# Moving operands at chosen offsets from the weights, modulo 128 bytes, in a two-layer fp32 block

## The chip, the cores and the metric

The kernel runs on one core of one Trainium2 chip. The time is the device time of one execution in microseconds; several executions are taken and the median is given. Profiled executions carry their own time, beside the span from their first to their last instruction.

## The reference

A block of two layers works on 256 tokens of 2048 features in float32; at the end stands an RMS norm. Layer 0 has a mixer with a convolution branch and a pooling branch, layer 1 a short-convolution mixer; each is followed by a SwiGLU of hidden size 5632. Cut to what matters:

```python
def conv_pool_mixer(x, ...):               # layer 0
    u = rms_norm(x, norm_g) @ w_in         # 2048 -> 3072
    a = a_val * sigmoid(a_gate)            # 1024 features: 31-tap causal convolution, layer norm, silu
    p = multiscale_pool(b_in, w_pool, ...) # 1024 features in four groups, four windows
    return concatenate([a, p]) @ w_out     # 2048 -> 2048

def short_conv_mixer(x, ...):              # layer 1
    u = rms_norm(x, norm_g) @ w_in         # 2048 -> 6144
    y = gate_b * causal_depthwise_conv(gate_c * v, conv_w)
    return y @ w_out                       # 2048 -> 2048

def swiglu(h, w_gate, w_up, w_down):       # 2048 -> 5632 (twice) -> 2048
    return (silu(h @ w_gate) * (h @ w_up)) @ w_down

for i in range(2):
    h = h + mixer_i(h)
    h = h + swiglu(rms_norm(h, ffn_norm[i]), w_gate[i], w_up[i], w_down[i])
return rms_norm(h, final_norm)
```

## The kernel before

Features lie on the 128 partitions, tokens along the free dimension (T = 256), so the weights are the stationary operand of each matmul and the activations the moving one. All weights are cut into blocks of 128 x 128 and stored in the order in which they are used. Units of 16 blocks come from HBM through one queue into the tile `w`; each piece of 8 blocks is then split into two fp32r tiles, `hi` by a cast on ScalarE (line 114) and `lo`, the rest, by a subtraction on VectorE or, in a part of the first mixer, on GpSimd (line 121). There are 4 buffers of `w`, and 6 each of `hi` and `lo`.

An activation is split in the same way: a chunk of 128 features takes 2 x 256 columns of fp32r, the high parts and then the low parts. The tiles that matmuls stream as moving operands are four. `xs` holds the normalised input of a layer part (16 chunks of 2048 bytes in each partition); it is one tile that every norm writes again. `cat` holds the two branches of the first mixer (8 chunks), `y` the hidden half of a SwiGLU (22 chunks), and `z` the gated product of the second mixer (16 chunks).

The product of one weight block and one chunk has two forms. The narrow one, used in the first mixer and in the last 22 blocks of all, is three matmuls of 256 columns, with `hi`, `hi` and `lo` as weights (lines 166 to 168); it is called a triple below. The wide one, used in all other parts, is a pair (lines 163 and 164):

```python
nc.tensor.matmul(acc, hi, x, ...)               # 512 columns
nc.tensor.matmul(acc[:, T:], lo, x[:, :T], ...) # 256 columns
```

Every matmul loads its own weights, so that a weight load stands ahead of each. TensorE follows the order of the program: the first mixer (`xs`, then `cat` through the pooling weights, `xs` and `cat` through the output weights), the first SwiGLU (twice: `xs`, then `y`), the second mixer (`xs`, then `z`), and the second SwiGLU (twice: `xs`, then `y`). Vector work and splits are put behind the products of the part before; a scheduler fixes the order on each engine when the program is built.

Tiles are laid out in each partition in the order of their pools. In the program as built, all buffers of `hi` and `lo` begin at 64 modulo 128 bytes, and a block within them is 512 bytes, so that every weight load begins there. `xs` (from byte 36160 of a partition) also begins at 64, `y` and `z` (from 159136) at 32, `cat` (from 184672) at 96; a chunk is a multiple of 128 bytes. The distance from the weights to the moving operand, modulo 128, is thus 0 for `xs`, 96 for `y` and `z`, and 32 for `cat`. This distance is called the offset below.

Of the kernel before, what the change touches and what calls it, by code (L numbers as in the profile page):

```python
# [12 lines left out]
F32R = mybir.dt.float32r  # L13
# [4 lines left out]
P = 128  # L18
T = 256
D = 2048  # L20
NC = D // P
DC = 1024
NA = DC // P
FF = 5632
NF = FF // P
NH = NF // 2
# [46 lines left out]
WARM = 9  # L73

KEEP = 8

POOL_SPLIT = range(96, 24 * NC + 16 + 7 * NC + 8)

# [6 lines left out]
def block_kernel(ctx: ExitStack, tc: tile.TileContext, xT: bass.AP, xtok: bass.AP, vec: bass.AP, wall: bass.AP, out: bass.AP):  # L85
    nc = tc.nc
    const = ctx.enter_context(tc.tile_pool(name="const", bufs=1))
    act = ctx.enter_context(tc.tile_pool(name="act", bufs=1))
# [35 lines left out]
    def next_block():  # L124
        b, i = cursor
        at = UNIT_AT[PIECES[i][0]] + PIECES[i][1]
        if b == at + PIECES[i][2]:
            ready.pop(i)
            i, at = i + 1, b
        for j in range(i, i + LOOK + 1):  # L130
            prepare(j)
        if i + LOOK < len(PIECES):
            for u in range(PIECES[i + LOOK][0] + 1, PIECES[i + LOOK][0] + AHEAD + 1):
                fetch(u)
        cursor[:] = [b + 1, i]
        hi, lo = ready[i]
        o = (b - at) * P
        return hi[:, o : o + P], lo[:, o : o + P]
# [8 lines left out]
    def tick():  # L147
        for name, q in queues.items():
            credit[name] = credit[name] + 1.0 if q else 0.0
            while q and credit[name] >= PACE[q[0][0]]:  # L150
                cost, step = q.popleft()
                credit[name] -= PACE[cost]
                step()

    def drain():
        while any(queues.values()):
            for q in queues.values():
                if q:
                    q.popleft()[1]()

    def product(acc, hi, lo, x, first, last, wide):
        if wide:
            nc.tensor.matmul(acc, hi, x, start=first, stop=False, skip_group_check=True)  # L163
            nc.tensor.matmul(acc[:, T:], lo, x[:, :T], start=False, stop=last, skip_group_check=True)  # L164
        else:
            nc.tensor.matmul(acc[:, :T], hi, x[:, :T], start=first, stop=False)  # L166
            nc.tensor.matmul(acc[:, :T], hi, x[:, T:], start=False, stop=False)  # L167
            nc.tensor.matmul(acc[:, :T], lo, x[:, :T], start=False, stop=last)  # L168

    def matmul_chunks(xs, ks, n=1, wide=False, behind=None):  # L170


        accs = [ps.tile([P, 2 * T], F32, name="acc") for _ in range(n)]
        for i, k in enumerate(ks):
            first, last = i == 0, i == len(ks) - 1
            for acc in accs:
                hi, lo = next_block()
                product(acc, hi, lo, xs[:, k, :], first, last, wide)
                tick()
            if behind is not None:  # L180
                behind(k)
        return accs
# [10 lines left out]
    def split(dst, src, scale=None):  # L193

        if scale is None:
            nc.scalar.copy(dst[:, :T], src)
            nc.vector.tensor_tensor(out=dst[:, T:], in0=src, in1=dst[:, :T], op=ALU.subtract)
        else:
            nc.scalar.activation(dst[:, :T], src, AF.Copy, scale=scale)
            nc.vector.scalar_tensor_tensor(out=dst[:, T:], in0=src, scalar=scale, in1=dst[:, :T], op0=ALU.mult, op1=ALU.subtract)  # L200
# [4 lines left out]
    def col(name, i):  # L205
        return v[:, VECS[name] + i : VECS[name] + i + 1]

    identity = v[:, VECS["identity"] :]
    h = act.tile([P, NC, T], F32, name="h")
    xs = act.tile([P, NC, 2 * T], F32R, name="xs")  # L210
    ones = const.tile([P, P], F32, name="ones")
    nc.gpsimd.memset(ones, 1.0)

# [14 lines left out]
    def rsqrt_of(*totals, scale, halves=False, st=None):  # L228
# [9 lines left out]
        if halves:  # L238

            idle = ps.tile([P, P], F32, name="idle", tag="acc")  # L240
            with tc.issue_after(mm.ins):
                for _ in range(KEEP):
                    nc.tensor.matmul(idle, ones, ones, start=True, stop=True)  # L243
# [27 lines left out]
    class Norm:  # L271


        def __init__(self, gain, final=False):
            self.gain, self.final = gain, final
            self.sums = []

        def add(self, c):
# [6 lines left out]

        def scale(self, c):
            if not self.final:
                split(xs[:, c, :], h[:, c, :], col(self.gain, c))

        def square(self, c):  # L290
            if c == 0:
# [16 lines left out]
    def project(src, ks, norm=None, wide=False, narrow_end=False):  # L308

        for n in range(NC):  # L310
            if narrow_end and n == NC - 1:
                wide = False
            (acc,) = matmul_chunks(src, ks, wide=wide)
            if wide:
                t = phase[0].tile([P, T], F32, name="cross", bufs=3)
                nc.scalar.copy(t, acc[:, T:])
                nc.vector.tensor_tensor(out=h[:, n, :], in0=h[:, n, :], in1=t, op=ALU.add)
            nc.vector.tensor_tensor(out=h[:, n, :], in0=acc[:, :T], in1=h[:, n, :], op=ALU.add)  # L318
            if norm is not None:
                norm.add(n)  # L320

    def scaled(acc, r, name, wide=False):
        if not wide:
            s = (phase[0] if name == "pv" else tmp).tile([P, T], F32, name=name, bufs=2)
            nc.vector.tensor_tensor(out=s, in0=acc[:, :T], in1=r, op=ALU.mult)
            return s
        s = summed(acc, name)
        nc.vector.tensor_tensor(out=s, in0=s, in1=r, op=ALU.mult)
        return s


    norm = Norm("mix_norm_e")
    nc.sync.dma_start(v[:, :NC], vec[:, :NC])

    def load(at, n):
# [30 lines left out]
    every = range(NC)  # L366
    with tc.tile_pool(name="m0", bufs=1) as m0, tc.tile_pool(name="ps_side", bufs=2, space=PSUM) as ps_side:
# [1 line left out]
        a_in = m0.tile([P, NA, pad + T], F32, name="a_in")  # L369
        nc.gpsimd.memset(a_in[:, :, :pad], 0.0)  # L370
        conv = m0.tile([P, NA, T], F32, name="conv")
        cat = m0.tile([P, NA, 2 * T], F32R, name="cat")
        total = m0.tile([P, 2, T], F32, name="total")

        sides, prods, state = {}, {}, {}
# [156 lines left out]

        project(xs, POOL_CHUNKS)
        drain()
        norm = Norm("ffn_norm0")
        project(cat, range(NA), norm)

    def swiglu(norm, following):
        with tc.tile_pool(name="ffn", bufs=1) as fp:
            phase[0] = fp  # L540
            y = fp.tile([P, NH, 2 * T], F32R, name="y")
            r = None
            for half in range(2):
                for f in range(NH):
                    (acc_g,) = matmul_chunks(xs, every, wide=True)
                    (acc_u,) = matmul_chunks(xs, every, wide=True)
                    if r is None:
                        r = norm.rstd()
                    gate = scaled(acc_g, r, "gate", True)
                    up = scaled(acc_u, r, "val", True)  # L550
                    nc.scalar.activation(gate, gate, AF.Silu)
                    nc.vector.tensor_tensor(out=up, in0=up, in1=gate, op=ALU.mult)
                    split(y[:, f, :], up)
                project(y, range(NH), following if half else None, wide=True, narrow_end=half and following.final)
# [1 line left out]
    x0.close()  # L556


    after = Norm("mix_norm_o")
    swiglu(norm, after)  # L560


    norm = Norm("ffn_norm1")
    with tc.tile_pool(name="m1", bufs=1) as m1:
        phase[0] = m1
        z = m1.tile([P, NC, 2 * T], F32R, name="z")
        pad = SW - 1
        r = None
        for c in range(NC):
            (acc_c,) = matmul_chunks(xs, every, wide=True)  # L570
            (acc_v,) = matmul_chunks(xs, every, wide=True)
            if r is None:
                r = after.rstd()
            cg = scaled(acc_c, r, "gate", True)
            vv = scaled(acc_v, r, "val", True)
            cv = m1.tile([P, pad + T], F32, name="cv", bufs=2)
            nc.gpsimd.memset(cv[:, :pad], 0.0)
            nc.vector.tensor_tensor(out=cv[:, pad:], in0=cg, in1=vv, op=ALU.mult)
            wc = VECS["conv_w_o"] + c * SW
            co = m1.tile([P, T], F32, name="co", bufs=2)  # L580
            nc.vector.tensor_scalar(out=co, in0=cv[:, :T], scalar1=v[:, wc : wc + 1], scalar2=None, op0=ALU.mult)
            for k in range(1, SW):
                nc.vector.scalar_tensor_tensor(out=co, in0=cv[:, k : k + T], scalar=v[:, wc + k : wc + k + 1], in1=co, op0=ALU.mult, op1=ALU.add)
            (acc_b,) = matmul_chunks(xs, every, wide=True)
            bg = scaled(acc_b, r, "pv", True)
            nc.vector.tensor_tensor(out=bg, in0=bg, in1=co, op=ALU.mult)
            split(z[:, c, :], bg)
        project(z, every, norm, wide=True)


    last = Norm("final_norm", final=True)
    swiglu(norm, last)
    halves = rsqrt_of(*last.sums, scale=1.0 / D, halves=True)
    with tc.tile_pool(name="fin", bufs=1) as fin:

# [90 lines left out]
```

## Time and profile before

| What | Value |
|---|---|
| Median of 3 runs | 2106.06 us (2105.8 to 2108.58) |
| Profiled execution: its own time | 2103.73 us |
| Its span, first to last instruction | 2102.0 us |
| TensorE matmul busy | 2079.1 us, 99% of the span |
| TensorE weight load busy | 1855.8 us, 88% |
| VectorE busy | 1383.4 us, 66% |
| ScalarE busy | 1060.9 us, 50% |
| GpSimd busy | 200.6 us, 10% |
| Granted TensorE clock, mean | 0.997 of full speed |
| From HBM | 391.39 MB, 187 GB/s over the span |

Matmuls are pipelined: the profile gives each a duration that overlaps that of the next (391 ns for 512 columns, of which the next matmul lets about 230 pass). What one costs in a dense stream is therefore read as its pitch, the time from its start to the start of the next one, from the view of instructions in order of time; or as the length of a stretch over the number of products in it.

### The profile page before, as it was taken

The page shows a single profiled execution, that of the slowest core. Times are in us where ns is not written, and L with a number is a line of the kernel's source. Part 1 is how long each engine was busy: PE and PEld are TensorE (multiplying, and loading weights), DVE is VectorE, ACT ScalarE, POOL GpSimd, SP SyncE. Part 2 cuts the span into 40 slices and gives each one's busy share as a digit, 9 for nine tenths or more (in the row PEclk, how much of TensorE's full clock was granted, in tenths as well). Part 3 has the DMA queues.
Part 4 walks back from the last instruction along what each step waited for, and adds up shares of the span by engine and source line. Part 5 has one row for each costly group of instructions (what it writes and reads, how often), then busy time and mean ns, then how long its engine had stood idle before and what let it go on. Part 6 is the DMA issues. An engine that isn't in the chain of part 4 may idle for free.

```text
span 2102.0 us, 31608 instructions
## 1 busy us (share of the span) xinstructions
PE 2079.1 (99%) x12584; PEld 1855.8 (88%) x12584; DVE 1383.4 (66%) x1979; ACT 1060.9 (50%) x1571; POOL 200.6 (10%) x180
## 2 busy tenths in 40 slices
PE   8999999999999999999999999999999999999998
PEld 8999988888888888888888888888888888888887
DVE  6888866666556666666777777666666556666654
ACT  7776654444444444454444445554444444444453
POOL 3985200000000000011000001100000000000011
PEclk9999999999999999999999999999999999999999
DMA  8554455555555555555555555555555555555551
GB/s 326 187 191 168 158 184 197 183 198 182 194 185 188 193 187 194 183 196 182 183 198 182 198 183 193 180 189 198 183 196 184 189 192 183 198 182 199 182 192 68
DMA packets 56884, 395.53 MB, mean 188 GB/s; under 512 B 6432, under 2 KB 7200, under 8 KB 9760
## 3 DMA queue, kind: packets, MB, share of 16 engines
q1 hardware_dynamic: 56736, 393.52, 52.4%
q8 instruction: 98, 1.61, 0.3%
q14 instruction: 50, 0.41, 0.1%
HBM read 391.39 MB, written 2.10 MB: 187 GB/s over the span
## 4 chain that ended last, share of the span: by engine, by line
PE 98%; DMA 1%; DVE 1%; ACT 0%; SPq 0%; issue 0%; DVEq 0%; ACTq 0%
PE acc L163 57%; PE acc L164 30%; PE acc L166 4%; PE acc L168 4%; PE acc L167 4%; DMA rows<-in_xtok 0%; DMA h<-in_xT 0%; DVE res L603 0%; ACT hi L114 0%; PE st L237 0%; PE st L268 0%; DVE lo L121 0%; SPq L104 0%; ACT conv L475 0%; PE idle L243 0%
## 5 line engine op out<-in xcount | busy, mean ns | idle before, releaser
L114 ACT CAST hi<-w 128x1024 fp32r<-128x1024 f32 (+1 forms) x740 | 776.1, 1050 | 975.3 <-PE acc L163 621.0
L121 DVE TENSOR_TENSOR lo<-w,hi 128x1024 fp32r<-128x1024 f32 (+1 forms) x691 | 845.2, 1224 | 639.5 <-ACT hi L114 635.3
L163 PE MATMUL acc<-xs,hi 128*128 128x512 f32 x3584 | 1243.3, 391 | 0.0
L164 PE MATMUL acc<-xs,lo 128*128 128x256 f32 x3584 | 1004.7, 280 | 0.0
L163 PEld LDWEIGHTS acc<-xs,hi 128*128 128x128 f32 x3584 | 670.4, 187 | 146.2
L164 PEld LDWEIGHTS acc<-xs,lo 128*128 128x128 f32 x3584 | 678.1, 189 | 0.1
L163 PE MATMUL acc<-y,hi 128*128 128x512 f32 x1386 | 485.2, 393 | 0.0
L164 PE MATMUL acc<-y,lo 128*128 128x256 f32 x1386 | 386.4, 279 | 0.0
L163 PEld LDWEIGHTS acc<-y,hi 128*128 128x128 f32 x1386 | 259.4, 187 | 61.7
L164 PEld LDWEIGHTS acc<-y,lo 128*128 128x128 f32 x1386 | 259.9, 187 | 0.4
L298 POOL TENSOR_TENSOR sumsq<-sumsq,sq 128x256 f32<-128x256 f32 x56 | 58.8, 1050 | 1599.1 <-ACT sq L296 1599.1
L166 PE MATMUL acc<-xs,hi 128*128 128x256 f32 x512 | 144.0, 284 | 5.2 <-ACT hi L114 4.2
L167 PE MATMUL acc<-xs,hi 128*128 128x256 f32 x512 | 143.6, 283 | 0.0
L168 PE MATMUL acc<-xs,lo 128*128 128x256 f32 x512 | 141.3, 284 | 0.1
L121 POOL TENSOR_TENSOR lo<-w,hi 128x1024 fp32r<-128x1024 f32 x49 | 118.7, 2441 | 43.1 <-PE acc L167 34.3
L166 PEld LDWEIGHTS acc<-xs,hi 128*128 128x128 f32 x512 | 98.1, 192 | 6.2 <-ACT hi L114 5.0
L167 PEld LDWEIGHTS acc<-xs,hi 128*128 128x128 f32 x512 | 98.2, 192 | 0.0
L168 PEld LDWEIGHTS acc<-xs,lo 128*128 128x128 f32 x512 | 96.5, 192 | 0.5 <-DVE lo L121 0.5
L163 PE MATMUL acc<-z,hi 128*128 128x512 f32 x256 | 89.6, 393 | 0.0
L188 ACT COPY cross<-acc 128x256 f32<-128x256 f32 x224 | 80.6, 360 | 0.0
L164 PE MATMUL acc<-z,lo 128*128 128x256 f32 x256 | 71.3, 279 | 0.0
L318 DVE TENSOR_TENSOR h<-acc,h 128x256 f32<-128x256 f32 x112 | 47.2, 423 | 18.9 <-PE acc L168 13.2
(134 smaller groups left out, 1198.6 us busy)
## 6 DMA issues: line engine op xcount, KB each, us to landing
w<-in_wall SPq DMA_DIRECT2D x365, 1024.0 KB, 4.8
w<-in_wall SPq DMA_DIRECT2D x7, 512.0 KB, 7.7
rows<-in_xtok SPq DMA_DIRECT2D x2, 1024.0 KB, 7.9
h<-in_xT SPq DMA_DIRECT2D x7, 256.0 KB, 7.3
out<-res SPq DMA_DIRECT2D x2, 512.0 KB, 2.8
out<-res SPq DMA_DIRECT2D x2, 384.0 KB, 2.8
v<-in_vec SPq DMA_DIRECT2D x1, 260.0 KB, 6.7
h<-in_xT SPq DMA_DIRECT2D x2, 128.0 KB, 2.3
```

Of the source, the lines that this page charges most:

```text
L114: nc.scalar.copy(hi[:, : n * P], w)
L121: engine.tensor_tensor(out=lo[:, : n * P], in0=w, in1=hi[:, : n * P], op=ALU.subtract)
L163: nc.tensor.matmul(acc, hi, x, start=first, stop=False, skip_group_check=True)
L164: nc.tensor.matmul(acc[:, T:], lo, x[:, :T], start=False, stop=last, skip_group_check=True)
L166: nc.tensor.matmul(acc[:, :T], hi, x[:, :T], start=first, stop=False)
L167: nc.tensor.matmul(acc[:, :T], hi, x[:, T:], start=False, stop=False)
L168: nc.tensor.matmul(acc[:, :T], lo, x[:, :T], start=False, stop=last)
L188: nc.scalar.copy(t, acc[:, T:])
L298: nc.gpsimd.tensor_tensor(out=self.sums[0], in0=self.sums[0], in1=sq, op=ALU.add)
L318: nc.vector.tensor_tensor(out=h[:, n, :], in0=acc[:, :T], in1=h[:, n, :], op=ALU.add)
```

## The change

Each moving tile becomes a room that is 32 fp32r elements (128 bytes) longer, and the operand is a view into it that begins 0, 32, 64 or 96 bytes in. `xs` stays one room, and each norm has its own view into it; the matmuls of a part take the view of that part's norm. `XS_M0`, `CAT` and so on are bytes.

```diff
+XS_M0 = 96
+XS_F0 = 32
+XS_M1 = 64
+XS_F1 = 0
+Y_F0 = 64
+Y_F1 = 32
+Z_M1 = 96
+CAT = 32
...
-    xs = act.tile([P, NC, 2 * T], F32R, name="xs")
+    xs_room = act.tile([P, NC * 2 * T + 32], F32R, name="xs")
+
+    def moving(room, at, n):
+
+        return room[:, at // 4 : at // 4 + n * 2 * T].rearrange("p (c t) -> p c t", c=n)
+
...
-        def __init__(self, gain, final=False):
+        def __init__(self, gain, at=0, final=False):
             self.gain, self.final = gain, final
+            self.xs = moving(xs_room, at, NC)
...
-                split(xs[:, c, :], h[:, c, :], col(self.gain, c))
+                split(self.xs[:, c, :], h[:, c, :], col(self.gain, c))
...
-    norm = Norm("mix_norm_e")
+    norm = Norm("mix_norm_e", XS_M0)
+    xs = norm.xs
...
-        cat = m0.tile([P, NA, 2 * T], F32R, name="cat")
+        cat = moving(m0.tile([P, NA * 2 * T + 32], F32R, name="cat"), CAT, NA)
...
-            y = fp.tile([P, NH, 2 * T], F32R, name="y")
+            y = moving(fp.tile([P, NH * 2 * T + 32], F32R, name="y"), at, NH)
...
-                    (acc_g,) = matmul_chunks(xs, every, wide=True)
-                    (acc_u,) = matmul_chunks(xs, every, wide=True)
+                    (acc_g,) = matmul_chunks(norm.xs, every, wide=True)
+                    (acc_u,) = matmul_chunks(norm.xs, every, wide=True)
...
-        z = m1.tile([P, NC, 2 * T], F32R, name="z")
+        z = moving(m1.tile([P, NC * 2 * T + 32], F32R, name="z"), Z_M1, NC)
```

Since the rooms are 128 bytes longer, all other tiles move by multiples of 128 bytes and keep their place modulo 128; the weights still begin at 64. The offsets, and how many products have each, are:

| Part | Operand | Products | Offset before | Offset now |
|---|---|---|---|---|
| first mixer | `xs` | 512 triples | 0 | 96 |
| first mixer | `cat` | 144 triples | 32 | 64 |
| first SwiGLU | `xs` | 1408 pairs | 0 | 32 |
| first SwiGLU | `y` | 704 pairs | 96 | 32 |
| second mixer | `xs` | 768 pairs | 0 | 64 |
| second mixer | `z` | 256 pairs | 96 | 64 |
| second SwiGLU | `xs` | 1408 pairs | 0 | 0 |
| second SwiGLU | `y` | 682 pairs, 22 triples | 96 | 0 |

No instruction is added, removed or moved: on all five engines the built program has the same instructions in the same order, with the same waits, before and after.

## Rows read from the trace of the kernel before

**Rows 1.** The page, parts 1 and 2: busy time by engine, clock in 40 slices.

```profile
PE 2079.1 (99%) x12584; PEld 1855.8 (88%) x12584; DVE 1383.4 (66%) x1979; ACT 1060.9 (50%) x1571; POOL 200.6 (10%) x180
...
PEclk9999999999999999999999999999999999999999
```

**Rows 2.** The page, part 4: shares of the chain that ended last.

```profile
PE 98%; DMA 1%; DVE 1%; ACT 0%; SPq 0%; issue 0%; DVEq 0%; ACTq 0%
```

**Rows 3.** The longest waits of TensorE: total, times, longest, in us.

```profile
PE acc L166 <- ACT hi L114: 4.2, 3, 1.7
PE acc L166 <- ACT cat L477: 3.4, 1, 3.4
PE st L268 <- DVE diag L260: 2.8, 1, 2.8
```

**Rows 4.** The page, part 5: the two splits of the weights, and what ends their idle time.

```profile
L114 ACT CAST hi<-w 128x1024 fp32r<-128x1024 f32 (+1 forms) x740 | 776.1, 1050 | 975.3 <-PE acc L163 621.0
L121 DVE TENSOR_TENSOR lo<-w,hi 128x1024 fp32r<-128x1024 f32 (+1 forms) x691 | 845.2, 1224 | 639.5 <-ACT hi L114 635.3
```

**Rows 5.** Instructions in order of time: five wide pairs that stream `xs`.

```profile
300.01 0.39 PE L163 MATMUL acc<-xs,hi 128*128 128x512 f32 x1
300.24 0.28 PE L164 MATMUL acc<-xs,lo 128*128 128x256 f32 x1
300.35 0.39 PE L163 MATMUL acc<-xs,hi 128*128 128x512 f32 x1
...
301.74 0.39 PE L163 MATMUL acc<-xs,hi 128*128 128x512 f32 x1
```

**Rows 6.** The same view: six wide pairs that stream `y`.

```profile
519.98 0.40 PE L163 MATMUL acc<-y,hi 128*128 128x512 f32 x1
...
522.08 0.39 PE L163 MATMUL acc<-y,hi 128*128 128x512 f32 x1
```

**Rows 7.** The same view: the first matmul of five stretches in a row of their kind.

```profile
628.13 0.40 PE L163 MATMUL acc<-xs,hi 128*128 128x512 f32 x1
...
872.19 0.40 PE L163 MATMUL acc<-y,hi 128*128 128x512 f32 x1
...
995.43 0.40 PE L163 MATMUL acc<-xs,hi 128*128 128x512 f32 x1
...
1263.03 0.40 PE L163 MATMUL acc<-z,hi 128*128 128x512 f32 x1
...
1352.67 0.40 PE L163 MATMUL acc<-xs,hi 128*128 128x512 f32 x1
```

**Rows 8.** The same view: three triples on `xs`, first mixer.

```profile
60.08 0.28 PE L166 MATMUL acc<-xs,hi 128*128 128x256 f32 x1
...
61.16 0.28 PE L166 MATMUL acc<-xs,hi 128*128 128x256 f32 x1
```

**Rows 9.** The same view: four triples on `cat`, first mixer.

```profile
230.07 0.28 PE L166 MATMUL acc<-cat,hi 128*128 128x256 f32 x1
...
231.47 0.28 PE L166 MATMUL acc<-cat,hi 128*128 128x256 f32 x1
```

**Rows 10.** The same view: three triples on `y`, the last 22 products.

```profile
2082.01 0.28 PE L166 MATMUL acc<-y,hi 128*128 128x256 f32 x1
...
2083.09 0.28 PE L166 MATMUL acc<-y,hi 128*128 128x256 f32 x1
```

**Rows 11.** The same view, weight loads alone, beside the pairs of rows 5.

```profile
300.01 0.19 PEld L164 LDWEIGHTS acc<-xs,lo 128*128 128x128 f32 x1
300.24 0.19 PEld L163 LDWEIGHTS acc<-xs,hi 128*128 128x128 f32 x1
```

**Rows 12.** Stretches on `xs`, `y`, line 163 alone: length, busy and count by engine, clock, DMA.

```profile
628.10:872.20 244.10, 244.10 (x706) 131.70 (x705) 1.00 0.54 190
872.20:995.40 123.20, 123.13 (x353) 65.85 (x353) 1.00 0.53 188
```

More of the change, by code (lines that the diff above doesn't have):

```diff
@@ L534, in block_kernel, with swiglu @@
         drain()
-        norm = Norm("ffn_norm0")
+        norm = Norm("ffn_norm0", XS_F0)
         project(cat, range(NA), norm)
-    def swiglu(norm, following):
+    def swiglu(norm, following, at):
         with tc.tile_pool(name="ffn", bufs=1) as fp:
             phase[0] = fp
-            y = fp.tile([P, NH, 2 * T], F32R, name="y")
+            y = moving(fp.tile([P, NH * 2 * T + 32], F32R, name="y"), at, NH)
             r = None
@@ L556, in block_kernel @@
     x0.close()
-    after = Norm("mix_norm_o")
-    swiglu(norm, after)
-    norm = Norm("ffn_norm1")
+    after = Norm("mix_norm_o", XS_M1)
+    swiglu(norm, after, Y_F0)
+    norm = Norm("ffn_norm1", XS_F1)
     with tc.tile_pool(name="m1", bufs=1) as m1:
         phase[0] = m1
-        z = m1.tile([P, NC, 2 * T], F32R, name="z")
+        z = moving(m1.tile([P, NC * 2 * T + 32], F32R, name="z"), Z_M1, NC)
         pad = SW - 1
@@ L569, in block_kernel @@
         for c in range(NC):
-            (acc_c,) = matmul_chunks(xs, every, wide=True)
-            (acc_v,) = matmul_chunks(xs, every, wide=True)
+            (acc_c,) = matmul_chunks(after.xs, every, wide=True)
+            (acc_v,) = matmul_chunks(after.xs, every, wide=True)
             if r is None:
@@ L583, in block_kernel @@
                 nc.vector.scalar_tensor_tensor(out=co, in0=cv[:, k : k + T], scalar=v[:, wc + k : wc + k + 1], in1=co, op0=ALU.mult, op1=ALU.add)
-            (acc_b,) = matmul_chunks(xs, every, wide=True)
+            (acc_b,) = matmul_chunks(after.xs, every, wide=True)
             bg = scaled(acc_b, r, "pv", True)
@@ L591, in block_kernel @@
     last = Norm("final_norm", final=True)
-    swiglu(norm, last)
+    swiglu(norm, last, Y_F1)
     halves = rsqrt_of(*last.sums, scale=1.0 / D, halves=True)
```

## The prediction

> **What bounds the kernel now.** I read the page's busy times and clock first. [...] Then the waits: the three longest of TensorE are 4.2, 3.4 and 2.8 us in all [rows 3], so nothing is to be had from other engines, and the engines that make the weights have room: the cast to `hi` idles for 975.3 us, 621.0 of it because TensorE has not yet freed a buffer [rows 4]. If TensorE gets faster by ten or twenty microseconds, ScalarE and VectorE are simply released earlier.
>
> The change leaves every instruction where it is. What it changes is the address at which TensorE's moving operand begins. So the question is whether a matmul's pitch depends on that address, and the trace of before can say so, because its four moving tiles stand at three offsets. The view to read is that of instructions in order of time, since the durations overlap.
>
> - Offset 0, wide: five pairs on `xs` take 301.74 - 300.01 = 1.73 us [rows 5]. Over a whole stretch: 872.19 - 628.13 = 244.06 us for 2 x 22 x 16 = 704 pairs [rows 7], **346.7 ns** a pair.
> - Offset 96, wide: six pairs on `y` take 2.10 us [rows 6]; the whole stretch takes 995.43 - 872.19 = 123.24 us for 352 pairs [rows 7], **350.1 ns**. On `z`: 1352.67 - 1263.03 = 89.64 us for 256 pairs [rows 7], 350.2 ns.
> - Offset 0, narrow: nine matmuls on `xs` in 61.16 - 60.08 = 1.08 us [rows 8], 120.0 ns each, **360 ns** a triple.
> - Offset 32, narrow: twelve matmuls on `cat` in 231.47 - 230.07 = 1.40 us [rows 9], 116.7 ns each, **350 ns** a triple.
> - Offset 96, narrow: nine matmuls on `y` in 1.08 us [rows 10], **360 ns** a triple.
>
> The same matmul with the same kind of weights thus has a pitch that depends on which tile it streams, at the same clock and DMA load [rows 12]. [...] The place of the tile can't be all of it: `cat` and `y` lie in the same upper part of the partition, `xs` far below, and narrow `y` goes with `xs`, not with `cat`. Each weight load starts within 0.01 us of the matmul ahead of the one it serves [rows 11], so weights and moving data are read side by side; that a distance between the two should matter fits this, though the rows show only the dependence, not its cause. I take the step as real and the offset as what sets it.
>
> **The change, part by part.** For each operand: products times the step.
>
> 1. Wide products that leave offset 96: `y` of the first SwiGLU (704 pairs), `z` (256), `y` of the second (682), together 1642. Brought to the pitch of offset 0 they gain 350.0 - 346.7 = 3.33 ns each: 1642 x 3.33 = 5.47 us. The 682 pairs of the second SwiGLU really go to 0 (2.27 us); that part is as good as measured. The other 960 go to 32 and 64 and are corrected in the next two steps.
> 2. Wide products at offset 32: 1408 on `xs` and 704 on `y`, 2112 pairs. No row shows a wide pair there. The ends come from the nearest rows: a gain of one step in both of its matmuls, as the narrow form shows between 0 and 32 (6.67 ns), and a loss of one step, as the wide form shows between 0 and 96 (3.33 ns). Which? At offset 0 the hi matmul of a pair has a pitch of 230 ns [rows 5], which leaves 346.7 - 230 = 116.7 for the lo one. That already stands where the narrow one gets to at 32; only the hi matmul can have a step left. I take one step: -3.33 ns, 2112 x 3.33 = **-7.04 us**. Ends: -14.08 and +7.04 us.
> 3. Wide products at offset 64: 768 on `xs`, 256 on `z`, 1024 pairs. No row of either form stands at 64; it lies 32 from the fast narrow offset and 32 from the slow wide one. I take **0** against offset 0, with the same two ends: -6.83 and +3.41 us.
> 4. The first mixer's `xs`, 512 triples from 0 to 96: the narrow rows at 0 and at 96 are equal, 360 ns, so **0**. The same holds for the last 22 triples, from 96 to 0.
> 5. `cat`, 144 triples from 32 to 64: it leaves the best narrow row for an offset without one. Two of the three measured offsets are slow, so I take the slow value: 144 x 10 ns = **+1.44 us**; the other end is 0.
> 6. ScalarE and VectorE write and TensorE reads views that begin elsewhere; the writes have the same lengths and stand in the same order, and with 975 us of idle time on ScalarE [rows 4] a write that took a little longer would still lie under TensorE's work. The second SwiGLU's `xs` stays at 0: nothing.
>
> Sum: -5.47 - 7.04 + 0 + 0 + 1.44 = **-11.07 us**. The profiled execution took 2103.73 us, 1.73 more than its span of 2102.0, and would take 2092.7. The median of the runs lies 2.33 us above that execution, so the forecast is 2106.06 - 11.07 = **2095.0 us**. With all ends on one side the sum is -5.47 - 14.08 - 6.83 = -26.4 us (2079.7), or -5.47 + 7.04 + 3.41 + 1.44 = +6.4 us (2112.5).
>
> [...]
>
> **The rivals.**
>
> - *Only the slow offset goes (B).* Wide pairs at 0, 32 and 64 are alike, and 96 is the one bad place. For it: at 0 the lo matmul is already at the best pitch seen, and 230 for twice as many columns is less than twice 116.7. Then -5.47 + 1.44 = -4.0 us, 2102.0; with `cat` unharmed -5.5, 2100.6.
> - *More steps than one (C).* A pair at 32 gains in both of its matmuls, as the narrow form does in each, and one at 64 in one. Then -5.47 - 14.08 - 3.41 = -23.0 us, 2083.1. Against it: the lo matmul would have to fall under every pitch of 256 columns in these rows.
> - *Offset 0 is the good place for wide pairs (D), slower.* Every other offset costs the step that 96 costs. Then 1408 + 768 pairs on `xs` rise from 346.7 to 350 (+7.25 us), the 960 on `y` and `z` stay as they are, the 682 gain 2.27, `cat` loses 1.44: +6.4 us, 2112.5. It turns to slower than before once the mean loss on those 2176 pairs passes (2.27 - 1.44) / 2176 = 0.4 ns. For it: 0 is the better of the two wide offsets that have rows; against it: 0 is among the slow ones in the narrow form.
> - *The offset modulo 128 is not what counts (E).* The tile's place in the partition, or its distance modulo something larger, sets the step. The tiles all keep their region, so nothing moves: 2106.1, give or take 1 us. [...] Against it: narrow `y` and `cat`, neighbours in place, differ by 10 ns a triple.
>
> **How the numbers follow.** Forecast 0.35, B 0.20, C 0.15, D 0.15, E 0.15. About 0.2%, 4.2 us, is what a measurement of this kernel can tell from no change. Faster by more: the forecast, C, and half of B, which lies on the boundary: 0.60. Within it: E and the other half of B: 0.25. Slower: D, 0.15. The range leaves out D and the outer part of C, together 0.2: 2083 to 2110 us. The forecast's own range, with `cat` at either value and step 3 off by half a step on its 1024 pairs, is 2091.5 to 2097.
>
> **What would show it.** In the profile of the changed kernel the lengths of stretches decide: 704 wide pairs on `xs` in the first SwiGLU should take 704 x 343.3 = 241.7 us instead of 244.1, and 352 on `y` 120.9 instead of 123.2; in the second mixer a pair should stay near 346.7 on `xs` and fall to it on `z`; in the second SwiGLU `xs` should be unchanged and `y` take 122.0 us for 352. A triple on `xs` should stay at 360 ns, on `cat` rise from 350 to 360. The prediction is wrong if wide pairs at 32 stand at 346.7 (B) or 350 (D), at 340 (C), or if `y` in the second SwiGLU stays at 350 (E). The last would also sink the reading by offsets itself.

## The result and the profile after

The changed kernel takes **2112.93 us** (median of 8 runs, 2112.14 to 2114.48) against 2105.79 before (8 runs, 2104.89 to 2108.58): a ratio of 1.0033, 95% interval 1.0022 to 1.0044. It is slower by 7.1 us; 2095.0, with a range of 2083 to 2110, was forecast.

The profiled execution took 2112.84 us with a span of 2111.1, 9.1 more than that of before. The mean granted clock is 0.997 of full speed in both, TensorE is still busy for 99%, and its longest waits are the same to within 1 us [rows 1, 3]. The page's first row of busy times:

```profile
PE 2088.0 (99%) x12584; PEld 1859.2 (88%) x12584; DVE 1383.6 (66%) x1979; ACT 1061.4 (50%) x1571; POOL 200.6 (10%) x180
```

Nearly all of the difference lies in the pitches of TensorE's matmuls. The first matmul of the stretches, in the view of instructions in order of time (line 173 is the hi matmul, which was 163); the answer to [rows 7]:

```profile
625.82 0.39 PE L173 MATMUL acc<-xs,hi 128*128 128x512 f32 x1
...
869.88 0.39 PE L173 MATMUL acc<-y,hi 128*128 128x512 f32 x1
...
991.92 0.39 PE L173 MATMUL acc<-xs,hi 128*128 128x512 f32 x1
...
1050.10 0.40 PE L173 MATMUL acc<-xs,hi 128*128 128x512 f32 x1
...
1052.22 0.40 PE L173 MATMUL acc<-xs,hi 128*128 128x512 f32 x1
...
1264.57 0.40 PE L173 MATMUL acc<-z,hi 128*128 128x512 f32 x1
...
1355.01 0.39 PE L173 MATMUL acc<-xs,hi 128*128 128x512 f32 x1
...
1603.51 0.39 PE L173 MATMUL acc<-y,hi 128*128 128x512 f32 x1
...
1727.08 0.39 PE L173 MATMUL acc<-xs,hi 128*128 128x512 f32 x1
...
1974.26 0.40 PE L173 MATMUL acc<-y,hi 128*128 128x512 f32 x1
```

- First SwiGLU, `xs`: 869.88 - 625.82 = 244.06 us for 704 pairs, 346.7 ns, as before. `y`: 122.04 us for 352, 346.7 ns; it was 350.1. A gain of 2.4 us in the two halves.
- Second mixer, `xs`: 2.12 us for six pairs, **353.3 ns** instead of 346.7; 768 pairs, a loss of 5.1 us. `z`: 90.44 us for 256, 353.3 instead of 350.2, 0.8 us.
- Second SwiGLU, `xs`: 1974.26 - 1727.08 = 247.18 us for 704, **351.1 ns** instead of 346.7; 1408 pairs, a loss of 6.2 us, in a part whose offset, modulo 128, had not changed. `y`: 1727.08 - 1603.51 = 123.57 us for 352, 351.1 instead of 350.1, 0.7 us.

And two stretches of the first mixer, 24 triples from the first row to the second in each, the answer to [rows 8, 9]:

```profile
60.01 0.28 PE L176 MATMUL acc<-xs,hi 128*128 128x256 f32 x1
...
68.53 0.28 PE L176 MATMUL acc<-xs,hi 128*128 128x256 f32 x1
...
230.11 0.28 PE L176 MATMUL acc<-cat,hi 128*128 128x256 f32 x1
...
238.59 0.28 PE L176 MATMUL acc<-cat,hi 128*128 128x256 f32 x1
```

A triple on `xs` takes 8.52 / 24 = 355.0 ns (360 before: 512 triples, -2.6 us), one on `cat` 8.48 / 24 = 353.3 (350 before: 144, +0.5 us). Sum: -2.4 + 5.1 + 0.8 + 6.2 + 0.7 - 2.6 + 0.5 = +8.3 of the 9.1 us. Most of the rest stands in the first mixer, where the wide part begins only 1.1 us earlier (258.4 against 259.5) instead of the 2.1 that the triples give. In both profiles the granted clock falls from 1.00 to 0.50 at 209.4 us, around two waits of TensorE (2.8 and 3.4 us [rows 3]), and is back at 1.00 some 6.5 us later. The triples on `cat` begin at 213.26 us before and at 210.73 now, so more matmuls meet the lower clock. The stretch at 0.50 around these waits (length, TensorE busy and its matmuls, clock, DMA), before and then after:

```profile
209.40:216.10 6.70, 3.31 (x15) 0.50 0.44 158
209.40:215.80 6.40, 5.07 (x23) 0.50 0.13 56
```

There they start 0.21 us apart instead of 0.12; 8 more of them cost, as an estimate, some 0.7 us.

The puzzle is the second SwiGLU. Modulo 128 its `xs` stands where it stood, and is slower by a pitch that no row of before had. One thing did change there: the room is 128 bytes longer, so the weights lie 128 bytes further from it. **Theory:** the pitch goes by the distance modulo 256. In these terms the change set `xs` to 224, 160, 192 and 128, `y` to 160 and 128, `z` to 192 and `cat` to 64, since its rooms of 32 elements move the weights by half a period. That also fits `xs` and `y` (160 and 160), `xs` and `z` (192 and 192), and `xs` and `y` (128 and 128) agreeing to 0.1 ns, though in each of these couples the two are 256 bytes apart modulo 512. **Rivals:** the period is 128 and the view or room costs something; or the address itself counts, of weights or operand.

### The profile page after: what moved, and what is told of

Its sections match the earlier page's. It is cut to its first block, busy times and chain, and to the rows that moved or that the text cites. A ratio compares the mean times of both kernels' runs of the same rounds, so it can differ in the third digit from the quotient of the medians.

```text
span 2111.1 us, 31608 instructions
## 1 busy us (share of the span) xinstructions
PE 2088.0 (99%) x12584; PEld 1859.2 (88%) x12584; DVE 1383.6 (66%) x1979; ACT 1061.4 (50%) x1571; POOL 200.6 (10%) x180
## 4 chain that ended last, share of the span: by engine, by line
PE 98%; DMA 1%; DVE 1%; ACT 0%; SPq 0%; issue 0%; DVEq 0%; ACTq 0%
PE acc L173 57%; PE acc L174 29%; PE acc L176 4%; PE acc L178 4%; PE acc L177 4%; DMA rows<-in_xtok 0%; DMA h<-in_xT 0%; DVE res L620 0%; ACT hi L124 0%; PE st L252 0%; DVE lo L131 0%; PE st L283 0%; SPq L114 0%; ACT conv L492 0%; PE idle L258 0%
```

## The experiments

Times of single runs stand beside the kernel before on the same chip; the pitches are read from each trace as above, between two starts 24 or 30 products apart. The numbers are those of the order in which the runs were made.

**Run 1. Rooms of 256 bytes.** The change with every `+ 32]` of a room made `+ 64]`, and nothing else.

```diff
-    xs_room = act.tile([P, NC * 2 * T + 32], F32R, name="xs")
+    xs_room = act.tile([P, NC * 2 * T + 64], F32R, name="xs")
```

> The rooms are 256 bytes longer instead of 128; the bytes at which the views begin stay as in the change. Modulo 128 every offset is that of the change; modulo 256 the offsets on xs become 96, 32, 64 and 0 (in the change 224, 160, 192 and 128), those on y, z and cat stay (160 and 128, 192, 64). Theory: the pitch goes by the offset modulo 256. Then xs of the second SwiGLU falls from 351 ns a pair back to 346.7 (1408 pairs, -6.2 us), y and z stay at 346.7, 351 and 353, and xs at 32 and 64 show new values. Rival 1, modulo 128 as the change has it: no pitch moves, 2112.9 us. Rival 2, the distance of 65536 bytes between xs and the weights in the kernel before was the good case, or a shifted view is slow in itself: xs of the second SwiGLU stays at 351.

2113.5 us (before: 2104.8). Three stretches on `xs`, each by two starts 30 pairs apart: the second mixer, then the first and the second half of the second SwiGLU:

```profile
1050.35 0.40 PE L173 MATMUL acc<-xs,hi 128*128 128x512 f32 x1
...
1060.95 0.40 PE L173 MATMUL acc<-xs,hi 128*128 128x512 f32 x1
...
1400.17 0.39 PE L173 MATMUL acc<-xs,hi 128*128 128x512 f32 x1
...
1410.57 0.39 PE L173 MATMUL acc<-xs,hi 128*128 128x512 f32 x1
...
1750.23 0.40 PE L173 MATMUL acc<-xs,hi 128*128 128x512 f32 x1
...
1760.83 0.40 PE L173 MATMUL acc<-xs,hi 128*128 128x512 f32 x1
```

At offset 0 the first half takes 10.40 / 30 = 346.7 ns, as the theory has it, but the second half, with the same addresses, 10.60 / 30 = 353.3. So modulo 128 falls, since 351.1 is gone with 128 bytes of room; and at offset 0 there is more than one pitch. `y` and `z`, whose distance modulo 256 stays while their addresses and the weights' move by 128, take 346.7, 351.1 and 353.3 as in the change. Offset 32 gives 346.7 on `xs`, 64 gives 353.3, and triples at 96 take 360 as on `y` before.

**Run 2. Everything 128 bytes higher.** The kernel before with one unused tile.

```diff
+    act.tile([P, 32], F32, name="gap")
     xs = act.tile([P, NC, 2 * T], F32R, name="xs")
```

> The kernel before with an unused tile of 128 bytes ahead of xs: moving operands and weights all lie 128 bytes higher, and every distance between them is as before. Theory (distance modulo 256): every pitch as before, 346.7 on xs, 350.1 on y and z, 120.0 and 116.7 narrow; 2105.8 us, within 1. Rival (the address itself counts, of the weights or of the moving operand, modulo 256): the weights now begin where they do in the changed kernel, and the pitches move: xs from 346.7 towards 351, some +6 to +15 us in all.

2118.3 us (before: 2104.8), and neither answer fits whole. All stretches on `y` and `z` take 350.0 ns, the triples 360 and 350, as before: the address alone does nothing there. But of five stretches on `xs`, all at offset 0, two take 346.7 ns and three 353.3 for most of their length. In the first of them, the rows on `xs` are 24 pairs apart, then 15, then 30. Between the sections stand short matmuls of the norm: eight of one column (line 238), then two on `diag` in the middle of a pair (line 269); the profile shows no wait of TensorE there.

```profile
262.36 0.40 PE L163 MATMUL acc<-xs,hi 128*128 128x512 f32 x1
...
270.84 0.40 PE L163 MATMUL acc<-xs,hi 128*128 128x512 f32 x1
...
271.90 0.50 PE L238 MATMUL st<-ones,sumsq 128*128 128x1 f32 x4
272.26 0.58 PE L238 MATMUL st<-ones,sq 128*128 128x1 f32 x4
...
274.18 0.39 PE L163 MATMUL acc<-xs,hi 128*128 128x512 f32 x1
...
279.38 0.40 PE L163 MATMUL acc<-xs,hi 128*128 128x512 f32 x1
...
279.96 0.60 PE L269 MATMUL st<-diag,ones 128*128 128x256 f32 x2
...
300.29 0.40 PE L163 MATMUL acc<-xs,hi 128*128 128x512 f32 x1
...
310.89 0.40 PE L163 MATMUL acc<-xs,hi 128*128 128x512 f32 x1
```

353.3, then 5.20 / 15 = 346.7, then 353.3 again, with the same operand and the same weight buffers. At offset 0 the stream has **two rhythms**; in all these traces it keeps one as long as pair follows pair, and it can come out of a break in either.

**Run 7. The same program again**, timed.

> The kernel of the second run again, all tiles 128 bytes higher, distances as before. It had three stretches on xs at 353 ns a pair instead of 346.7, two at 346.7, at one and the same offset 0. Theory (at offset 0 the stream has two steady rhythms, and a stall at the start of a stretch decides which is held): over executions the time takes values 4.6 to 5 us apart between 2105 and 2120, as each stretch falls into one or the other, or always the same one where the stalls repeat exactly. Rival (the address counts after all): always 2118, with the same stretches slow.

2118.85 us (2118.02 to 2119.32), ratio 1.0063 with an interval of 1.0047 to 1.0080. The same three stretches are slow in this execution, but the short sections at the start of the first are not those of run 2:

```profile
262.24 0.40 PE L163 MATMUL acc<-xs,hi 128*128 128x512 f32 x1
...
270.56 0.40 PE L163 MATMUL acc<-xs,hi 128*128 128x512 f32 x1
...
274.25 0.40 PE L163 MATMUL acc<-xs,hi 128*128 128x512 f32 x1
...
279.55 0.40 PE L163 MATMUL acc<-xs,hi 128*128 128x512 f32 x1
```

346.7 and 353.3, where run 2 had 353.3 and 346.7, in one and the same program. So the rhythm is not a matter of the program's addresses alone. The long stretches repeat all the same, as the rival has it, but the theory allows for that too: the times alone decide nothing here. By how much: 704 + 768 + 704 pairs at 6.6 ns are 14 us, the whole of the 13.6 us to before.

**Run 3. Other offsets on other tiles.** Rooms of 256 bytes, other numbers in the table.

```diff
-XS_M0 = 96
-XS_F0 = 32
-XS_M1 = 64
-XS_F1 = 0
-Y_F0 = 64
-Y_F1 = 32
-Z_M1 = 96
-CAT = 32
+XS_M0 = 32
+XS_F0 = 224
+XS_M1 = 96
+XS_F1 = 160
+Y_F0 = 192
+Y_F1 = 160
+Z_M1 = 224
+CAT = 224
```

> Rooms of 256 bytes as in the first run, other bytes for the views, so that offsets modulo 256 are: first mixer xs 32, cat 0; first SwiGLU xs 224, y 32; second mixer xs 96, z 64; second SwiGLU xs 160, y 0. Theory (distance modulo 256 alone, whichever tile it is): triples on xs at 32 take 350 ns as cat did, on cat at 0 360 as xs did; pairs on xs at 96 take 350.1 as y did, on xs at 160 346.7, on y at 0 346.7; y at 32 and z at 64 agree with xs at 32 and 64 of the first run; xs at 224 is new. Rival (the tile or its region counts too): the same offset gives another pitch on another tile.

2113.8 us (before: 2104.8). `xs` at 32 takes 350 ns a triple as `cat` did, `cat` at 0 360 as `xs` did; pairs on `xs` at 96 350.0, at 160 346.7; on `y` at 32 346.7; on `z` at 64 353.3; on `xs` at 224 353.3. `y` at 0 began its first half at 353.3, went to 346.7 after 25 pairs and took 353.3 in its second half: the two rhythms again on another tile. The change stands at 1616.9 us, where two hi matmuls follow each other and then two lo, without a wait or a foreign matmul. Where an offset has one pitch, the tile does not count; the distance does.

**Run 8. Offsets between.** The same with `XS_M0` 48, `CAT` 240, `XS_F0` 16, `Y_F0` 208, `XS_M1` 40, `Z_M1` 184, `XS_F1` 144, `Y_F1` 80.

> Offsets between the multiples of 32, modulo 256: first mixer xs 48, cat 16; first SwiGLU xs 16, y 48; second mixer xs 40, z 24; second SwiGLU xs 144, y 176. Theory (the step is 32 bytes, what lies inside one gives the pitch of its beginning): pairs at 16 and 24 as at 0 (346.7 or 353.3), at 40 and 48 346.7 as at 32, at 144 351.1 as at 128, at 176 346.7 as at 160; triples at 48 350, at 16 360. [...]

2110.0 us in one run (before: 2105.2, the median of 7). Pairs take 346.7 at 16 and 144, 355.6 at 24, 353.3 at 40, 350.0 at 48 and 176. So there is no step of 32 bytes inside which the pitch holds: 24 and 40 are among the slowest, beside 32, which is among the fastest. With hi and lo alike, all runs and both kernels together give, in ns:

| Offset modulo 256 | Pair | Triple |
|---|---|---|
| 0 | 346.7 or 353.3 | 360 |
| 16 | 346.7 | 356 |
| 24 | 355.6 | |
| 32 | 346.7 | 350 or 353 |
| 40 | 353.3 | |
| 48 | 350.0 | 355 |
| 64 | 353.3 | 353 |
| 96 | 350.0 | 360 |
| 128 | 351.1 | 356 |
| 144 | 346.7 | |
| 160 | 346.7 | 352 or 360 |
| 176 | 350.0 | 358 |
| 192, 224 | 353.3 | at 224: 355 |

Modulo 128 still holds for much of it: pairs at 16 and 144, 32 and 160, 48 and 176, 64 and 192 agree. It is 0 against 128, 96 against 224, and the triples, that tell 128 bytes apart.

**Run 4. The lo buffers moved alone**, by 64 bytes; the kernel before, `xs` and hi where they were.

```diff
     whl = ctx.enter_context(tc.tile_pool(name="whl", bufs=6))
+    gap = ctx.enter_context(tc.tile_pool(name="gap", bufs=1))
+    gap.tile([P, 16], F32, name="gap")
+    wlo = ctx.enter_context(tc.tile_pool(name="wlo", bufs=6))
...
-        lo = whl.tile([P, PIECE * P], F32R, name="lo")
+        lo = wlo.tile([P, PIECE * P], F32R, name="lo")
```

> The kernel before with the lo buffers 64 bytes higher, in a pool of their own behind an unused tile of 64 bytes; hi buffers and xs stay. So on xs the distance to hi is 0 and to lo 192 modulo 256. Theory: a matmul is slowed by the weight load that runs beside it, which is that of the next matmul. Then in a wide pair on xs the hi matmul, beside which lo is loaded, takes 235 ns as at 192 in the changed kernel, and the lo matmul 116.7 as at 0: about 351.7 a pair. Rival: a matmul's own weights count. Then hi 230 and lo 118.5, about 348.5. If neither distance matters: 346.7.

2108.7 us (before: 2104.8). In the first mixer, 24 triples on `xs`:

```profile
60.10 0.28 PE L169 MATMUL acc<-xs,hi 128*128 128x256 f32 x1
...
68.58 0.28 PE L169 MATMUL acc<-xs,hi 128*128 128x256 f32 x1
```

8.48 / 24 = 353.3 ns, where before had 360 [rows 8]. The moving operand has not moved, nor have two of the three weights: where the weights of the third lie changes the pitch. So it is not the operand's own place that counts; and since a shift of everything leaves the triples alone (run 2), it is a distance in which these weights take part. Pairs on `xs` stayed at 346.7, which neither of the two forms of the theory gave. The move took `y` and `z` along, to 160 from hi and 96 from lo: their pairs rose from 350 to 353.3, and the last triples on `y` fell from 360 to 346.7 (21 of them in 7.28 us).

**Runs 9 and 10. lo moved by 32 and by 128 bytes**, with rooms of 256 bytes and the offsets as the expectations list them.

> Rooms of 256 bytes, and the lo buffers 32 bytes higher modulo 256, so that the offset to lo is 32 less than that to hi. Offsets to hi, lo: first mixer xs 32, 0, cat 64, 32; first SwiGLU xs 64, 32, y 32, 0; second mixer xs 0, 224, z 96, 64; second SwiGLU xs 160, 128, y 192, 160. With hi and lo alike, pairs took 346.7 at 32 and 160, 353.3 at 64, 192 and 224, 350.1 at 96, 351.1 at 128. Theory: the offset to the weights that are loaded beside the 512 columns (lo) decides: 346.7 on xs of the first SwiGLU and y of the second (lo at 32 and 160), more than 350 on xs of the second mixer and of the second SwiGLU (lo at 224 and 128). Rival: the offset to hi decides: 346.7 on xs of the second SwiGLU and y of the first, 353.3 on xs of the first SwiGLU and y of the second. Third: both together give values of their own.

> Rooms of 256 bytes, and the lo buffers 128 bytes higher modulo 256. Offsets to hi, lo: first mixer xs 32, 160, cat 0, 128; first SwiGLU xs 32, 160, y 0, 128; second mixer xs 64, 192, z 96, 224; second SwiGLU xs 160, 32, y 128, 0. If 128 bytes counted for nothing, as the change has it, every pitch is that of the same offset with hi and lo alike: 346.7 at 32 and 160, 353.3 at 64. Theory (lo decides, modulo 256): 346.7 at 32, 160 and at 160, 32; 353.3 at 64, 192; 353.3 at 96, 224; 351.1 at 0, 128; 346.7 or 353.3 at 128, 0. Rival (hi decides): 350.1 at 96, 224, 351.1 at 128, 0.

Pairs, as offset to hi, offset to lo: 64, 32: 348.9; 32, 0: **344.5**; 0, 224: 346.7; 96, 64: 353.3; 160, 128: 351.1 and 350.7; 192, 160: 353.3; 32, 160: 346.7; 0, 128: 346.7; 64, 192: 346.7; 96, 224: 350.0; 160, 32: 350.0; 128, 0: 352.0. Neither the hi nor the lo offset decides: 64 gives 353.3 with 64, 348.9 with 32 and 346.7 with 192. The third answer is right; both together give values of their own. And 128 bytes count: 64, 192 and 64, 64 are 6.6 ns apart. 344.5 ns lies below 346.7, the lowest pitch of a pair up to then. The single runs took 2112.9 and 2107.5 us (before: one run of 2110.3). That run of before lies 4.5 us above the median of 2105.8; one stretch of 704 pairs in the slower rhythm would cost about as much, but the execution has no profile, so this is not shown.

**Run 11. Nudges at offset 0.** The kernel before with a few useless matmuls inside the second half of each SwiGLU.

```diff
                 for f in range(NH):
+                    if half and f in NUDGES:
+                        nudge = ps_st.tile([P, P], F32, name="nudge", tag="st")
+                        nc.tensor.matmul(nudge[:, : NUDGES[f]], ones, ones[:, : NUDGES[f]], start=True, stop=True)
                     (acc_g,) = matmul_chunks(xs, every, wide=True)
```

> The kernel before with six small extra matmuls in the second half of each SwiGLU, on xs at offset 0: ahead of gate blocks 3, 6, 9, 12, 15 and 18 one of 16, 32, 48, 64, 96 and 128 columns of ones, whose result nobody reads. Nothing else is added; a nudge should cost well under 1 us. Theory (two steady rhythms at offset 0, and a disturbance picks one): between nudges the pitch holds one value, and after some of the nudges it is 353.3 instead of 346.7 for the whole of the next 96 pairs. Rival (the rhythm is set by addresses or by the stretch): 346.7 in all seven sections.

The pitch is 346.7 in every one of the sections between the nudges; 30 pairs, between the second and the third nudge:

```profile
700.21 0.39 PE L165 MATMUL acc<-xs,hi 128*128 128x512 f32 x1
...
710.61 0.39 PE L165 MATMUL acc<-xs,hi 128*128 128x512 f32 x1
```

The single run took 2107.6 us (before: 2110.3). None of the twelve nudges changed the rhythm, so in this form the theory failed. But the same execution does change it elsewhere, in the first stretch on `xs`, which stands ahead of any nudge: 24 pairs, then the one-column matmuls of the norm, and 30 pairs behind them:

```profile
262.28 0.40 PE L165 MATMUL acc<-xs,hi 128*128 128x512 f32 x1
...
270.76 0.40 PE L165 MATMUL acc<-xs,hi 128*128 128x512 f32 x1
...
271.82 0.50 PE L239 MATMUL st<-ones,sumsq 128*128 128x1 f32 x4
...
285.30 0.39 PE L165 MATMUL acc<-xs,hi 128*128 128x512 f32 x1
...
295.70 0.39 PE L165 MATMUL acc<-xs,hi 128*128 128x512 f32 x1
```

8.48 / 24 = 353.3 ns, then 10.40 / 30 = 346.7. So the changes of rhythm inside a stretch, here and in runs 2, 3 and 7, stand where the order of pairs is broken, and at none of them does the profile show a wait of TensorE. Why some breaks change it and the nudges, all of them met in the faster rhythm, did not, stays open.

**Run 5. The changed kernel with other numbers.** Rooms of 128 bytes as in the change.

```diff
-XS_M0 = 96
+XS_M0 = 32
-XS_M1 = 64
-XS_F1 = 0
+XS_M1 = 32
+XS_F1 = 32
-Y_F1 = 32
-Z_M1 = 96
-CAT = 32
+Y_F1 = 64
+Z_M1 = 64
+CAT = 0
```

> The changed kernel with other numbers in its table alone: every offset is 160 modulo 256 (32 modulo 128), cat's is 32. Theory (modulo 256; 160 is a fast wide offset that locks into one pitch): all pairs at 346.7 ns, so the second mixer loses the 6.6 and the second SwiGLU the 4.4 ns a pair that they cost in the change, and y and z gain 3.4 on the kernel before: 1642 x 3.4 = -5.6 us on before, and the first mixer between -2.6 (triples at 355) and -5.1 us (at 350): 2095 to 2098 us. Rival (the room or the shifted view costs something itself): above 2100 us.

**2096.36 us** (2095.68 to 2098.8), ratio 0.9959, interval 0.9944 to 0.9974. All pairs take 346.7 ns. The triples at 160 take 352 in the first stretch of `xs` and 360 in the second, so 160 too has two rhythms in the narrow form. The views and rooms cost nothing; the numbers did.

**Run 6. Every offset 32 modulo 256**, rooms of 256 bytes.

> Rooms of 256 bytes, every offset 32 modulo 256. Theory: all pairs at 346.7 ns, all triples at 350: on before 1642 x -3.4 = -5.6 us for y and z, 512 x -10 = -5.1 us for the first mixer's xs, nothing on the wide xs: 2095 us, faster than both kernels. Rival (offset 32 also has a second, slower state that a stall can start, as offset 0 has): some stretches at 353, each 704 pairs at 6.6 ns or 4.6 us more, 2099 to 2110.

**2095.53 us** (2093.77 to 2097.24), ratio 0.9953, interval 0.9938 to 0.9968. All pairs at 346.7, so for them the rival did not show. In the narrow form it did: the first stretch of `xs` took 350.0 ns a triple, the second, at the same offset, 353.3:

```profile
170.26 0.28 PE L176 MATMUL acc<-xs,hi 128*128 128x256 f32 x1
...
178.74 0.28 PE L176 MATMUL acc<-xs,hi 128*128 128x256 f32 x1
```

8.48 / 24 = 353.3. In run 11 `cat`, also at 32, took 353.3 as well, where the kernel before had 350 [rows 9].

**Run 12. The best pair of distances everywhere**: rooms of 256 bytes, lo 32 bytes higher, every offset 32 to hi and 0 to lo.

> Rooms of 256 bytes and the lo buffers 32 bytes higher, with every offset 32 to hi and 0 to lo modulo 256. In the ninth run pairs on y took 344.5 ns there, 2.2 less than at 32 to both, and triples 351.4, 1.2 more than at 32 to both. Theory (the two distances set the pitch, whatever the tile): 344.5 on all 5226 pairs, -11.5 us against all offsets at 32 (2095.5), +0.8 us for 656 triples: about 2085 us. Rival (344.5 belongs to y, or holds only as one of two rhythms): xs at 346.7 or 353, 2090 us or more.

**2083.64 us** (2082.85 to 2086.1), ratio 0.9904, interval 0.9887 to 0.9921. 30 pairs on `xs` in the first SwiGLU, then 30 on `y`:

```profile
300.29 0.39 PE L176 MATMUL acc<-xs,hi 128*128 128x512 f32 x1
...
310.62 0.39 PE L176 MATMUL acc<-xs,hi 128*128 128x512 f32 x1
...
530.05 0.39 PE L176 MATMUL acc<-y,hi 128*128 128x512 f32 x1
...
540.38 0.39 PE L176 MATMUL acc<-y,hi 128*128 128x512 f32 x1
```

10.33 / 30 = 344.4 ns on both. This version beats both kernels: by 21 us the one before, by 29 the change.

## Why the prediction was wrong

- *What bounds the kernel* was right. TensorE's pitches make the time [rows 1, 2] and give 8.3 of the 9.1 us, they depend on the distance from weights to moving operand, and no other engine's work showed up: TensorE's longest waits are the same to within 1 us. That the offset and not the tile's place sets the step was right too (runs 1, 3, 4). Rival E fell: in every layer part some pitch moved, and only `xs` of the first SwiGLU kept its own. (Though all 40 slices show 9 tenths or more [rows 1], the granted clock was 0.50 for 6.7 us from 209.4 us on. No row that the sum uses lies there.)
- *The sum failed in three terms of like size.* It missed the change of the span by 20 us, -11.07 against +9.1. By the pitches above, 7.0 us of that are step 2 (offset 32), 6.8 us step 3 (offset 64) and 9.2 us the second SwiGLU of steps 1 and 6; steps 4 and 5 erred the other way, by 3.5 us. The sum's step is, by its rows, 350.0 - 346.7 = 3.33 ns a wide pair and 120.0 - 116.7 a narrow matmul; that pitches differ by whole steps, as its ends take it, was an assumption that the runs do not bear out: 355.6, 351.1 and 344.5 ns (runs 8 and 9, the change) lie 8.9, 4.4 and -2.2 ns from 346.7.
- *The reading of "offset" failed.* The prediction took over the change's modulo 128. The period that fits all runs is 256, and the longer rooms had moved the weights by half of it. The rows of before could not show this: their three offsets, 0, 32 and 96, are the same in both counts. The fact was there, 128 bytes more in each room, and was passed over because all tiles "keep their place modulo 128". E named "modulo something larger", but concluded that then nothing moves. This explains the second SwiGLU and step 4, but not steps 2 and 3: run 1, where `xs` stands at 96, 32, 64 and 0 modulo 256 as the table of the change has it, was still 8.7 us slower than before.
- *Step 1*, "that part is as good as measured", and the line that the second SwiGLU's `xs` stays at 0 with no cost: these failed by the most. Both are at 128 modulo 256. In place of 0 and -2.27 us stand +6.2 and +0.7.
- *Step 3* (64 against 0 taken as nothing, ends -6.83 and +3.41): +6.6 ns on 768 pairs of `xs`, outside its upper end, and 353.3 on `z`. The end was set by the one wide step that rows showed, and two steps were possible. At a true 64 the pair takes 353.3 too (runs 1 and 3).
- *Step 2* (32): the pair takes 346.7 at 32 and at 160, so 0 in place of -3.33 ns on 2112 pairs. In this part alone B was right. The reading that hi "can have a step left" was half true: averaged over the starts of some 500 pairs on `xs` between 300 and 480 us of each trace, the hi matmul went from 230.0 ns before to 228.3 in run 6, but the lo one from 116.7 to 118.3, so that the pair kept 346.7.
- *Steps 4 and 5*: 355 in place of 360 on `xs`, as it stood at 224 and not at 96; 353.3 in place of 360 on `cat`. Both better than taken, by 2.6 and 0.9 us.
- *D came out at 2112.5 us for another reason.* Its mechanism, that every wide offset but 0 costs the step, is false: 160 costs nothing, and the second SwiGLU lost at what D counted as 0.
- *Offset 0 was taken as one pitch.* It has two, and the kernel before happens to hold the better in all the long stretches of its profiled execution [rows 5, 7]; run 2 kept every distance and lost 13.5 us.
- *That a distance between weights and moving operand should matter* was argued from loads that start beside the running matmul [rows 11]. The place of the weights does count: moving the lo weights alone by 64 bytes took a triple from 360 to 353.3 ns (run 4). Whether it is the read of the memory in which the two meet, and which of the two weight loads meets which matmul, no run shows.

Open: what sets the rhythm when the order of pairs is broken, and a model that gives the pitch from the two distances. The runs settle that distances count and how much; their order is only a table. A common shift of weights and operands was tried only by 128 bytes and its multiples, and hi begins at 64 modulo 128 in every run; that the addresses themselves count as well, modulo 128, is not excluded.

## What to carry to other kernels

When TensorE is the bound and a weight load stands ahead of each matmul, read its pitch stretch by stretch: two tiles with the same matmul and different pitches were the sign here that addresses cost time, up to 3% of a pair (344.4 to 355.6 ns) and 1% of the kernel (2083.64 us against 2104.55 before, run 12). Measure the residues instead of inferring them, count the distance from weights to moving operand after every tile has been laid out, and don't assume the period; a pad that keeps one period can break a longer one, as the 128 bytes of the rooms did (351.1 ns in place of 346.7). Prefer distances at which all stretches and executions hold one pitch, and move the weights' buffers as well as the moving operand: 344.4 and 344.5 ns came only with both moved (runs 9 and 12).

## What the runs showed of the hardware that was not expected

- The pitch of an fp32r pair (512 and 256 columns), in executions with a mean granted clock of 0.995 to 0.998, lies between 344.4 and 355.6 ns, that of a triple between 350 and 360 where hi and lo stand alike (346.7 at 160 from hi and 96 from lo, run 4), by the distances from hi and lo weights to the moving operand; the pattern fits a period of 256 bytes and has structure below 32 (346.7 at 16, 355.6 at 24, run 8).
- At one distance and one set of addresses two pitches can hold, 346.7 and 353.3 at offset 0, for hundreds of pairs. The one gave way to the other at short foreign matmuls of the norm (runs 2, 7 and 11) and once where two hi matmuls followed each other (run 3), without a wait; an inserted matmul of 16 to 128 columns did not bring it about. Triples have it too: 350 or 353.3 at 32 (run 6), 352 or 360 at 160 (run 5).
- The three long slow stretches fell the same way in both profiled executions of one program, the short sections did not (runs 2 and 7).
